# Holding nine instead of five groups of stores behind the loads, with smaller input pools and two groups of K and V in fp32

## The chip, the cores and the metric

The kernel runs on one core of a Trainium2 chip. The metric is the device time of one execution in microseconds; medians of several executions are quoted. A profile gives the span from the core's first to its last instruction, which here is about 1.8 us shorter than the time of the same execution (129.08 against 130.87 us). A ratio always compares with the kernel before as it ran in the same rounds on the same chip; the rounds used several chips.

The names: PE multiplies matrices, DVE and ACT work on vectors, POOL and SP here mostly issue DMA transfers. A DMA issued by POOL stands in the profile under a queue of the kind "software_dynamic"; one issued by SP or ACT under "hardware_dynamic", called a hardware queue below. The profile counts the packets of all queues against the same 16 DMA engines. The traces have sixteen reports of each transfer, read here as one for each engine; a transfer has landed with the last of them.

## The reference, cut to what matters

```python
# Q, K, V: (8, 12, 512, 64) float32
Q_feat = np.maximum(0, Q)
K_feat = np.maximum(0, K)
KV    = np.einsum('bhkd,bhkv->bhdv', K_feat, V)
K_sum = np.sum(K_feat, axis=2)
numerator   = np.einsum('bhqd,bhdv->bhqv', Q_feat, KV)
denominator = np.einsum('bhqd,bhd->bhq', Q_feat, K_sum)
return numerator / (denominator[:, :, :, None] + 1e-10)
```

There are 96 heads in 24 groups of four. A group needs three loads (Q, K, V) of 512 KB each and one store of 512 KB. That is 72 loads and 24 stores, 50.3 MB in all, and little arithmetic per byte.

## The kernel before

The loads are all issued by POOL, and they convert fp32 in HBM to bf16 in SBUF on the way. The exceptions are K and V of group 0, which come unconverted over the hardware queues so that the first group can start early. Stores are issued by SP as soon as a group's result o_sb is ready, except for five groups (17 to 21), whose stores stand in POOL's program after the last load.

```python
HELD = 5
qin = pool("qin", NG); kin = pool("kin", 20); vin = pool("vin", 20)
outp = pool("outp", 10)
# ... cut ...
k_sb[0] = outp.tile([P, R, D], fp32, name="k_first", tag="o_sb")
nc.sync.dma_start(out=k_sb[0]..., in_=Kr[0])
v_sb[0] = outp.tile([P, R, D], fp32, name="v_first", tag="o_sb")
nc.scalar.dma_start(out=v_sb[0]..., in_=Vr[0])
load_q(0)                                  # POOL, as all of load_q, load_kv
make_identity(nc, ident)
for g in range(1, NG - 2):
    load_kv(g); load_q(g)
load_kv(NG - 2); load_kv(NG - 1); load_q(NG - 2); load_q(NG - 1)
# ... cut ...
def store(g, o_sb):
    if NG - 2 - HELD <= g < NG - 2:
        nc.gpsimd.dma_start(out=Or[g], in_=...)      # POOL: behind the loads
    elif g == NG - 1:
        for j in range(2):                           # SP: two halves of 256 KB
            nc.sync.dma_start(...)
    else:
        nc.sync.dma_start(out=Or[g], in_=...)        # SP: at once
```

Of the kernel before, what the change touches and what calls it, by code (L numbers as in the profile page):

```python
# [10 lines left out]
def kernel(  # L11
# [7 lines left out]
    nc = tc.nc  # L19
    B, H, S, D = Q.shape  # L20
    assert D == 64
    P = 128
# [4 lines left out]
    R = S * NHG // P  # L27
    U = R // 2
    NG = NH // NHG
    assert NG * NHG == NH and R == 16  # L30
    HELD = 5

    fp32 = mybir.dt.float32
    bf16 = mybir.dt.bfloat16
# [3 lines left out]
    def pool(name, bufs, **kw):  # L38
        return ctx.enter_context(tc.tile_pool(name=name, bufs=bufs, **kw))

    consts = pool("consts", 1)
    qin = pool("qin", NG)
    kin = pool("kin", 20)
    vin = pool("vin", 20)
    kfp = pool("kfp", 3)
    qtp = pool("qtp", 3)
    rcp = pool("rcp", 4)
    outp = pool("outp", 10)
    pkv = pool("pkv", 1, space=bass.MemoryType.PSUM)
    pqt = pool("pqt", 2, space=bass.MemoryType.PSUM)  # L50
    pou = pool("pou", 2, space=bass.MemoryType.PSUM)
# [1 line left out]
    def rview(X):  # L53
        return X.rearrange("b h s d -> (b h s d)").rearrange("(n p f) -> n p f", p=P, f=R * D)

    Qr, Kr, Vr, Or = rview(Q), rview(K), rview(V), rview(out)
# [13 lines left out]
    q_sb, k_sb, v_sb = {}, {}, {}  # L70

    def load_kv(g):
        k_sb[g] = kin.tile([P, R, D], bf16, name="k_sb")
        nc.gpsimd.dma_start(out=k_sb[g].rearrange("p r d -> p (r d)"), in_=Kr[g])  # L74
        v_sb[g] = vin.tile([P, R, D], bf16, name="v_sb")
        nc.gpsimd.dma_start(out=v_sb[g].rearrange("p r d -> p (r d)"), in_=Vr[g])  # L76

    def load_q(g):
        q_sb[g] = qin.tile([P, U, 2 * D], bf16, name="q_sb")
        nc.gpsimd.dma_start(out=q_sb[g].rearrange("p u f -> p (u f)"), in_=Qr[g])  # L80


    k_sb[0] = outp.tile([P, R, D], fp32, name="k_first", tag="o_sb")
    nc.sync.dma_start(out=k_sb[0].rearrange("p r d -> p (r d)"), in_=Kr[0])
    v_sb[0] = outp.tile([P, R, D], fp32, name="v_first", tag="o_sb")
    nc.scalar.dma_start(out=v_sb[0].rearrange("p r d -> p (r d)"), in_=Vr[0])
    load_q(0)
    make_identity(nc, ident)
    for g in range(1, NG - 2):
        load_kv(g)  # L90
        load_q(g)
    load_kv(NG - 2)
# [79 lines left out]
    def store(g, o_sb):  # L172
        if NG - 2 - HELD <= g < NG - 2:
            nc.gpsimd.dma_start(out=Or[g], in_=o_sb.rearrange("p r d -> p (r d)"))  # L174
        elif g == NG - 1:
            for j in range(2):
                rs = slice(R // 2 * j, R // 2 * (j + 1))
                nc.sync.dma_start(out=Or[g].rearrange("p (r d) -> p r d", d=D)[:, rs],
                                  in_=o_sb[:, rs])
        else:  # L180
            nc.sync.dma_start(out=Or[g], in_=o_sb.rearrange("p r d -> p (r d)"))
# [47 lines left out]
```

## Time and profile before

| | kernel before |
|---|---|
| time, median | 131.06 us (130.79 to 131.24, 3 runs) |
| span of the profiled run | 129.1 us |
| DMA share of the chain of waits | 86% |
| busy: DVE, PE, ACT | 62%, 59%, 40% |

From the profile page of the kernel before: the DMA engines' busy share in tenths, in 40 equal slices of 3.2 us, then the GB/s that they wrote.

```profile
DMA  4999999999999999999999999999999999999972
GB/s 118 305 209 209 211 171 274 277 219 285 229 269 272 226 285 250 245 286 239 258 282 225 275 262 234 285 249 248 285 230 267 273 227 206 212 216 368 388 307 111
```

From the same page, the chain of work that ended last, shares of the span.

```profile
DMA 86%; issue 3%; PE 3%; POOL 2%; DVE 2%; ACT 2%; ACTq 0%; POOLq 0%
```

The kernel is bound by the DMA engines, which have no hole until the last two slices. GB/s count bytes written; a load writes bf16, half of what it reads. So 209 means 418 GB/s read from HBM, and 388 near the end means stores.

Windows of the kernel before: start and end in us, length, busy time of the engines (with instruction counts), granted PE clock, mean DMA share, GB/s. The DMA share adds the times of overlapping packets, so about 1.0 to 1.1 is full.

```profile
5.00:16.00 11.00, 6.20 (x176) 5.21 (x176) 7.23 (x19) 5.21 (x14) 5.59 (x10) 0.98 1.12 210
118.00:122.00 4.00, 3.48 (x79) 2.75 (x76) 2.69 (x10) 2.29 (x6) 0.53 (x1) 0.59 1.02 408
122.00:124.00 2.00, 0.64 (x32) 0.46 (x32) 1.31 (x4) 0.79 (x1) 0.00 (x0) 1.00 0.70 285
124.00:125.00 1.00, 0.00 (x0) 0.00 (x0) 0.93 (x4) 0.00 (x0) 0.00 (x0) 0.87 0.90 365
125.00:126.00 1.00, 0.00 (x0) 0.00 (x0) 0.47 (x1) 0.00 (x0) 0.00 (x0) 0.50 0.74 293
126.00:127.00 1.00, 0.00 (x0) 0.00 (x0) 0.00 (x0) 0.00 (x0) 0.00 (x0) 0.50 0.76 291
```

The first line is loads alone, the second stores, with the end of the last load (it lands at 118.84). From 122 us on the engines are no longer full: they wait for the last groups' results. That slack is what the change is after. A pair of POOL's issues, ten groups apart, gives the price of a group in the middle (timeline; start us, us, engine, line, operation, tile, count, what the engine waited for):

```profile
39.37 0.53 POOL L74 DMA_DIRECT2D k_sb<-in_K_dram  x1 [0.51 <-DMA v_sb<-in_V_dram]
90.39 0.53 POOL L74 DMA_DIRECT2D k_sb<-in_K_dram  x1 [0.57 <-DMA v_sb<-in_V_dram]
```

That is 5.10 us for three loads and one store.

Now the end. From the list of DMA issues of the kernel before: tile, queue, count, KB each, median us from issue to landing.

```profile
out_dram<-o_sb SPq DMA_DIRECT2D x18, 512.0 KB, 6.9
out_dram<-o_sb POOLq DMA_DIRECT2D x5, 512.0 KB, 9.6
```

And the waits of SP's own queue in the kernel before (who waited for whom, us in total, times, longest). L224 is the line where the kernel ends: SP waits there for all landings, then for the other engines.

```profile
SPq L224 <- DMA out_dram<-o_sb: 1.4, 3, 0.6
SPq L224 <- PEq L224: 1.1, 2, 0.6
```

(PEq is PE's sequencer.)

### The profile page before, as it was taken

Reading aid. Unit: us, or ns where it says so; the run is one execution under the profiler, and the core shown is the slowest. Engines: PE = TensorE matmul, PEld = TensorE weight load, DVE = VectorE, ACT = ScalarE, POOL = GpSimd, SP = SyncE. Lnnn points to the kernel's source line nnn. Section 1 sums busy time; section 2 is a strip of 40 time slices with the busy share of each in tenths; the row PEclk is TensorE's granted clock in tenths of the full one; section 3 lists DMA queues with packets and bytes.
Section 4 is the critical chain, followed back from the end, with each engine's and each line's share of the span. In section 5 each row is a group of like instructions: output and inputs, shape, how many; then the busy total and the mean of one; then the engine's idle time right before and its main releaser. Section 6 shows DMA issues by size and latency. Waiting matters only on the chain.

```text
span 129.1 us, 4091 instructions
## 1 busy us (share of the span) xinstructions
PE 76.5 (59%) x1728; PEld 57.0 (44%) x1728; DVE 79.8 (62%) x230; ACT 51.1 (40%) x121; POOL 45.1 (35%) x81
## 2 busy tenths in 40 slices
PE   0068476547576585485675755855756458887610
PEld 0057354425444363364454544633644336665410
DVE  1283775737757558467476584584673849889660
ACT  3027535433345334433543453344335253652700
POOL 6945343133333315224333243152331335311100
PEclk9999955555555555555555555555555555555785
DMA  4999999999999999999999999999999999999972
GB/s 118 305 209 209 211 171 274 277 219 285 229 269 272 226 285 250 245 286 239 258 282 225 275 262 234 285 249 248 285 230 267 273 227 206 212 216 368 388 307 111
DMA packets 13986, 32.23 MB, mean 250 GB/s; under 512 B 1553, under 2 KB 1553, under 8 KB 13969
## 3 DMA queue, kind: packets, MB, share of 16 engines
q0 software_dynamic: 10800, 20.98, 81.7%
q1 hardware_dynamic: 3024, 10.49, 21.7%
q10 hardware_dynamic: 144, 0.52, 1.1%
q8 instruction: 13, 0.21, 0.6%
q14 instruction: 5, 0.03, 0.1%
HBM read 37.75 MB, written 12.58 MB: 390 GB/s over the span
## 4 chain that ended last, share of the span: by engine, by line
DMA 86%; issue 3%; PE 3%; POOL 2%; DVE 2%; ACT 2%; ACTq 0%; POOLq 0%
DMA q_sb<-in_Q_dram 38%; DMA k_sb<-in_K_dram 27%; DMA v_sb<-in_V_dram 21%; ACT qt L139 2%; PE ps_qt L135 1%; PE ps_out L150 1%; DVE o_sb L164 1%; POOL q_sb L80 0%; POOL v_sb L76 0%; POOL k_sb L74 0%; DVE rec L163 0%; POOL ident masks.py:199 0%; DVE den L161 0%; POOL ident masks.py:197 0%; ACTq L139 0%
## 5 line engine op out<-in xcount | busy, mean ns | idle before, releaser
L120 PE MATMUL ps_kv<-vo,kf 64*128 64x65 bf16 x768 | 25.1, 239 | 36.3 <-DVE vo L112 34.4
L120 PEld LDWEIGHTS <-kf 64*128 64x128 bf16 x768 | 21.4, 126 | 42.0 <-DVE vo L112 34.3
L129 ACT CAST kvd<-ps_kv 64x130 bf16<-64x130 f32 x96 | 25.3, 264 | 36.1 <-PE ps_kv L120 34.2
L139 ACT ACTIVATE qt<-ps_qt 128x1024 bf16<-128x1024 bf16 x24 | 24.6, 1023 | 33.8 <-PE ps_qt L135 33.8
L110 DVE TENSOR_SCALAR kf<-k_sb,mask 128x1024 bf16<-128x1024 bf16 x46 | 20.3, 483 | 27.2 <-DMA k_sb<-in_K_dram 27.2
L150 PE MATMUL ps_out<-kvd,qt 128*32 128x130 bf16 x768 | 28.8, 303 | 10.0 <-DVE o_sb L164 6.9
L164 DVE TENSOR_TENSOR o_sb<-ps_out,rec 128x512 f32<-128x512 f32 x48 | 33.2, 692 | 1.7
L80 POOL DMA_DIRECT2D q_sb<-in_Q_dram x24 | 17.2, 715 | 36.0 <-DMA k_sb<-in_K_dram 34.7
L150 PEld LDWEIGHTS <-qt 128*32 128x32 bf16 x768 | 17.4, 127 | 18.8 <-DVE o_sb L164 12.5
L135 PE MATMUL ps_qt<-ident,q_sb 128*128 128x128 bf16 x192 | 24.3, 306 | 0.7 <-DMA q_sb<-in_Q_dram 0.7
L135 PEld LDWEIGHTS <-q_sb 128*128 128x128 bf16 x192 | 18.1, 139 | 5.5 <-issue 4.4
L76 POOL DMA_DIRECT2D v_sb<-in_V_dram x23 | 12.3, 533 | 19.3 <-DMA q_sb<-in_Q_dram 15.0
L74 POOL DMA_DIRECT2D k_sb<-in_K_dram x23 | 12.4, 541 | 11.8 <-DMA v_sb<-in_V_dram 8.9
L112 DVE COPY vo<-v_sb 128x1024 bf16<-128x1024 bf16 x23 | 9.9, 431 | 8.5 <-DMA v_sb<-in_V_dram 8.5
L163 DVE RECIPROCAL rec<-den 128x8 f32<-128x8 f32 x48 | 9.7, 203 | 1.7
L161 DVE TENSOR_SCALAR den<-ps_out 128x8 f32<-128x8 f32 x48 | 7.5, 157 | 1.7 <-PE ps_out L150 1.7
L174 POOL DMA_DIRECT2D out_dram<-o_sb x5 | 2.7, 549 | 7.8 <-DVE o_sb L164 6.2
L110 DVE TENSOR_SCALAR kf<-k_first,mask 128x1024 bf16<-128x1024 f32 x2 | 1.4, 751 | 3.8 <-DMA k_first<-in_K_dram 3.8
L129 ACT ACT_TABLE_LOAD x1 | 1.3, 1283 | 1.8 <-DVE kvd L103 1.8
L101 DVE MEMSET mask<- 32x1 f32 x8 | 0.3, 59 | 0.9 <-PEq L213 0.8
L103 DVE MEMSET kvd<- 128x260 f32 x3 | 0.8, 275 | 0.0
L112 DVE CAST vo<-v_first 128x1024 bf16<-128x1024 f32 x1 | 0.7, 692 | 0.0
(7 smaller groups left out, 1.1 us busy)
## 6 DMA issues: line engine op xcount, KB each, us to landing
out_dram<-o_sb SPq DMA_DIRECT2D x18, 512.0 KB, 6.9
q_sb<-in_Q_dram POOLq DMA_DIRECT2D x24, 256.0 KB, 12.4
k_sb<-in_K_dram POOLq DMA_DIRECT2D x23, 256.0 KB, 13.7
v_sb<-in_V_dram POOLq DMA_DIRECT2D x23, 256.0 KB, 13.7
out_dram<-o_sb POOLq DMA_DIRECT2D x5, 512.0 KB, 9.6
v_first<-in_V_dram ACTq DMA_DIRECT2D x1, 512.0 KB, 4.8
k_first<-in_K_dram SPq DMA_DIRECT2D x1, 512.0 KB, 4.7
out_dram<-o_sb SPq DMA_DIRECT2D x2, 256.0 KB, 2.4
```

The costliest lines, as they stand in the source:

```text
L74: nc.gpsimd.dma_start(out=k_sb[g].rearrange("p r d -> p (r d)"), in_=Kr[g])
L76: nc.gpsimd.dma_start(out=v_sb[g].rearrange("p r d -> p (r d)"), in_=Vr[g])
L80: nc.gpsimd.dma_start(out=q_sb[g].rearrange("p u f -> p (u f)"), in_=Qr[g])
L110: nc.vector.tensor_scalar(kf[g][:, :, s, :], k_sb[g], scalar1=0.0, scalar2=mask[:, s:s + 1], op0=Alu.max, op1=Alu.mult)
L112: nc.vector.tensor_copy(vo[g % NB][:, :, 0:D], v_sb[g])
L120: nc.tensor.matmul(ps_kv[g][:, t, 0:D1], kf[g][ts_, r, :, :].rearrange("p s d -> p (s d)"), vo[g % NB][ts_, r, :], start=(r == 0), stop=(r ...
L129: nc.scalar.copy(kvd[g % NB][64 * c:64 * c + 64, :, s, c, :], ps_kv[g][64 * s:64 * s + 64, :, 0:D1])
L135: nc.tensor.transpose(ps_qt[g][:, u, :], q_sb[g][:, u, :], ident)
L139: nc.scalar.activation(qt[g].rearrange("p u q -> p (u q)"), ps_qt[g].rearrange("p u q -> p (u q)"), Act.Relu)
L150: nc.tensor.matmul(po[hs, v // 2, (v % 2) * 2 * D1:(v % 2) * 2 * D1 + 2 * D1], qt[g][:, u, hs], kvd[g % NB][:, h // 2, h % 2, :, :], start ...
L163: nc.vector.reciprocal(rec, den)
L164: nc.vector.tensor_tensor(o_sb[:, 8 * j:8 * j + 8].rearrange("p (b r) d -> p b r d", b=2), pv[:, :, :, 0:D], rec.unsqueeze(3).to_broadcast ...
```

## The change

Its intent: the time from 122 us on, in which the DMA engines wait for the last results, is to be filled with stores that are ready. So four more groups of stores (13 to 21 instead of 17 to 21) are held behind the loads. The loads end earlier, compute ends earlier, and the held stores cover the wait. Output buffers for this are won by smaller input pools. K and V of group 1 are also loaded in fp32 over the hardware queues.

```diff
-    HELD = 5
+    HELD = 9
+    F32 = 2
...
-    qin = pool("qin", NG)
-    kin = pool("kin", 20)
-    vin = pool("vin", 20)
+    qin = pool("qin", 14)
+    kin = pool("kin", 14)
+    vin = pool("vin", 14)
...
-    outp = pool("outp", 10)
+    outp = pool("outp", HELD + 4)
...
-    k_sb[0] = outp.tile([P, R, D], fp32, name="k_first", tag="o_sb")
-    ... (K[0] on SP, V[0] on ACT)
+    for g in range(F32):
+        ... (the same for g = 0 and 1)
     load_q(0)
     make_identity(nc, ident)
-    for g in range(1, NG - 2):
+    load_q(1)
+    for g in range(2, NG - 2):
         load_kv(g)
         load_q(g)
```

More of the change, by code (lines that the diff above doesn't have):

```diff
@@ L80, in load_q @@
         nc.gpsimd.dma_start(out=q_sb[g].rearrange("p u f -> p (u f)"), in_=Qr[g])
-    k_sb[0] = outp.tile([P, R, D], fp32, name="k_first", tag="o_sb")
-    nc.sync.dma_start(out=k_sb[0].rearrange("p r d -> p (r d)"), in_=Kr[0])
-    v_sb[0] = outp.tile([P, R, D], fp32, name="v_first", tag="o_sb")
-    nc.scalar.dma_start(out=v_sb[0].rearrange("p r d -> p (r d)"), in_=Vr[0])
+    for g in range(F32):
+        k_sb[g] = outp.tile([P, R, D], fp32, name="k_first", tag="o_sb")
+        nc.sync.dma_start(out=k_sb[g].rearrange("p r d -> p (r d)"), in_=Kr[g])
+        v_sb[g] = outp.tile([P, R, D], fp32, name="v_first", tag="o_sb")
+        nc.scalar.dma_start(out=v_sb[g].rearrange("p r d -> p (r d)"), in_=Vr[g])
     load_q(0)
     make_identity(nc, ident)
-    for g in range(1, NG - 2):
+    load_q(1)
+    for g in range(2, NG - 2):
         load_kv(g)
```

## The prediction

> **What bounds the kernel now.** The DMA engines. The slice table shows them at 9 tenths or more from about 3 us to 122 us, with no hole; the chain of waits is 86% DMA, all of it loads of Q, K and V. DVE (62%), PE (59%) and ACT (40%) have room. Cutting the span into 1 us windows gives the prices. Before the first store (5 to 16 us) 209 GB/s are written into SBUF; a load reads fp32 and writes bf16, so 420 GB/s are read, and one load (512 KB read) takes 1.25 us; POOL's issues there are also 1.24 us apart. In the middle a group (three loads, one store) takes 5.10 us (issues of K from 39.4 to 90.4 us, ten groups), so a mixed-in store costs 5.10 - 3.75 = 1.35 us. Stores alone (118 to 122 us) run at about 408 GB/s, 1.29 us each.
>
> So the time is nearly a sum: 72 loads and 24 stores at full rate, plus three losses: the start (by 3 us only 0.28 MB has moved, about 2.3 us lost), the tail, and about 2 us between the last byte (127.1) and the end of the span. In the tail the loads' data ends near 117 us, five held stores run to 122, then from 122 to 127.1 the DMA share is only 0.67 to 0.90 while stores wait for the last two groups' compute (last o_sb at 125.5). Seven stores and 1.5 loads take 12.1 us from 115 us on; at full rate about 10.9. Tail loss: 1.2 to 1.5 us. That is what the change can win.
>
> **What it removes, adds, moves.** No byte of HBM traffic is removed. Four more stores (groups 13 to 16) move behind the loads: loads end 4 x 1.35 = 5.4 us earlier (about 111.5), so the last o_sb is ready near 120 to 121 us; eleven stores then follow, 11 x 1.29 = 14.1 us, to about 125.6. The backlog covers the last groups' compute with some 4 us to spare, so the tail loss should nearly vanish. The moved stores cost 1.29 instead of 1.35 us: 0.25 us more. In the longer load-only stretch DMA needs 3.75 us per group, and DVE needs 3.7 (prep to prep, 105 to 116 us), so compute just keeps pace; a small lag is covered.
>
> 14 input buffers: POOL keeps just 8 transfers outstanding (each issue waits for the landing of the eighth before it), under three groups ahead, so neither 20 nor 14 binds. 13 output buffers: no o_sb waits for a held store.
>
> K1 and V1 in fp32: same bytes read, so about the same DMA time. The Trainium skill (DMA: Bandwidth & Descriptors, "Issuing engines are not separate DMA queues") says all queues share the same 16 engines; this trace agrees: adding SP's stores slows the loads. Gain at the start at most 0.3 us. Cost: group 1's prep is about 0.8 us longer on DVE (751 against 482 ns twice, 692 against 430), hidden.
>
> **Predicted:** span about 127.5, time 129.4 us (-1.3%), range 128.5 to 130.5. Faster by over 2%: 0.10; within 2%: 0.87; slower: 0.03.
>
> **What would show it right:** load-only stretch from about 75 us on at 209 GB/s; last load landing about 5 us earlier; then some 13 us of stores near 400 GB/s at full DMA share; chain of waits ending in a store's DMA instead of DVE o_sb; middle still 5.1 us per group.
>
> **What would make it wrong:** stores alone slower than 400 GB/s when many are queued, or POOL's eight-deep window starving them; DVE not keeping 3.7 us, so that last stores come after 125 us; fp32 loads on hardware queues moving faster or slower than cast loads; a larger gain at the start than 0.3 us.

## The result, and the profile after

| | before | changed |
|---|---|---|
| time, median | 130.93 us (4 runs) | 133.09 us (132.86 to 133.19, 4 runs) |
| span of the profiled run | 129.1 us | 131.3 us |
| ratio to before | | 1.016, 95% interval 1.0134 to 1.0186 |

A ratio is the mean time of one kernel's fast runs over that of the other's of the same rounds, so it is not quite the ratio of the medians quoted. The changed kernel is 1.6% slower, clear of the noise, where 1.3% faster had been predicted. It stays within 2% of the kernel before, to which the prediction gave 0.87, but with the opposite sign and outside the range of 128.5 to 130.5 us, so this is no success of its argument. (The median before is over one run more than in the table above.)

The same slices of the changed kernel (each 3.3 us now):

```profile
DMA  4999999999999999999999999999999999999920
GB/s 119 376 291 209 212 182 280 275 238 270 252 240 283 248 248 284 237 258 273 237 270 264 232 285 255 240 210 210 210 209 210 209 213 240 401 411 418 393 91 0
```

Much of what was planned happened. There is a long stretch of loads alone near 210 GB/s, then stores alone at 393 to 418, with DMA engines full. But the last slice holds no DMA at all, and the one before it little. The windows of the changed kernel show it:

```profile
112.00:124.00 12.00, 5.04 (x112) 3.95 (x112) 5.72 (x16) 3.08 (x6) 1.60 (x3) 0.50 1.03 413
124.00:125.00 1.00, 0.00 (x0) 0.00 (x0) 0.00 (x0) 0.00 (x0) 0.00 (x0) 0.50 0.73 289
125.00:126.00 1.00, 0.00 (x0) 0.00 (x0) 0.00 (x0) 0.00 (x0) 0.00 (x0) 0.50 0.44 174
126.00:127.00 1.00, 0.00 (x0) 0.00 (x0) 0.00 (x0) 0.00 (x0) 0.00 (x0) 0.50 0.15 57
127.00:128.40 1.40, 0.00 (x0) 0.00 (x0) 0.00 (x0) 0.00 (x0) 0.00 (x0) 0.50 0.00 0
128.40:131.00 2.60, 0.00 (x0) 0.00 (x0) 0.00 (x0) 0.00 (x0) 0.00 (x0) 0.50 0.00 0
```

Twelve microseconds at 413 GB/s are what was hoped for. Then two things follow that the prediction did not have. The DMA share decays over 3 us (0.73, 0.44, 0.15) instead of stopping, which means that some of the 16 engines finish much later than others. And from 127.3 us on nothing moves, no engine is busy, and yet the program goes on to 131.25. The waits of SP's queue in the changed kernel (L227 is the end of the kernel):

```profile
SPq L227 <- DMA out_dram<-o_sb: 6.6, 1, 6.6
SPq L227 <- PEq L227: 3.3, 2, 2.8
```

SP waits for the last landing and then 2.8 us more for the other engines, against 0.6 before. PEq is only the name nearest in time: PE had long finished. The trace's own records of the sequencers name the engine that is late. At its end the program has a DRAIN instruction on each engine (prof leaves it out of its views; these times were read from the packed traces). POOL's is the long one: in the changed kernel it begins with POOL's last issue and runs for 15.5 us, against 1.0 us or less on the others:

```
kernel     POOL's last issue   POOL's last landing   POOL's DRAIN ends   SP is done   span
before     119.71              125.19                128.29              127.92       129.08
changed    114.98              127.28                130.46              127.83       131.25
```

(All in us. "SP is done" is the end of SP's DRAIN after its waits for all landings.) In both kernels the span is the later of the two columns before it plus 0.79 us. In the kernel before, POOL's drain already ends last, but only by 0.37 us. In the changed kernel POOL's drain ends 2.6 us after SP is done, and the whole difference of the spans (2.17 us) is the difference of the drains' ends (2.17 us). In these two kernels the drain ends 3.1 to 3.2 us after the last landing on POOL's own queue.

Why does POOL's queue land so late? Its last store was issued early. The last of POOL's held stores in the changed kernel (all operations on the output that start between 114.5 and 115.5 us):

```profile
L177 POOL DMA_DIRECT2D out_dram<-o_sb x1: 533/533/533, 115.0 to 115.0; - x1
DMA to landing us min/median/max: 12.3/12.3/12.3
```

And the last of them in the kernel before (between 119 and 120 us):

```profile
L174 POOL DMA_DIRECT2D out_dram<-o_sb x1: 531/531/531, 119.7 to 119.7; - x1
DMA to landing us min/median/max: 5.5/5.5/5.5
```

With nine held stores and those of the last groups behind the loads, all of this work ends together near 127 us, so POOL's queue, too, lands at the very end. With five it was through 2.5 us before SP's last piece.

### The profile page after: what moved, and what is told of

Same layout as the page of the kernel before. It is cut to its first block, busy times and chain, and to the rows that moved or that the text cites. A ratio compares the mean times of both kernels' runs of the same rounds, so it can differ in the third digit from the quotient of the medians.

```text
span 131.3 us, 4110 instructions
## 1 busy us (share of the span) xinstructions
PE 76.9 (59%) x1728; PEld 57.2 (44%) x1728; DVE 80.2 (61%) x230; ACT 51.3 (39%) x121; POOL 44.6 (34%) x83
## 4 chain that ended last, share of the span: by engine, by line
DMA 76%; DVE 4%; PE 4%; POOL 3%; issue 3%; ACT 2%; ACTq 0%; POOLq 0%
DMA v_sb<-in_V_dram 39%; DMA k_sb<-in_K_dram 20%; DMA q_sb<-in_Q_dram 17%; DVE o_sb L167 2%; ACT qt L142 2%; PE ps_qt L138 2%; PE ps_out L153 1%; POOL k_sb L75 1%; DVE vo L115 1%; PE ps_kv L123 1%; POOL q_sb L81 1%; DVE kf L113 1%; DVE rec L166 0%; POOL v_sb L77 0%; DVE den L164 0%
## 5 line engine op out<-in xcount | busy, mean ns | idle before, releaser
L113 DVE TENSOR_SCALAR kf<-k_sb,mask 128x1024 bf16<-128x1024 bf16 x44 | 19.4, 483 | 18.4 <-DMA k_sb<-in_K_dram 18.4
L81 POOL DMA_DIRECT2D q_sb<-in_Q_dram x24 | 15.6, 648 | 31.5 <-DMA k_sb<-in_K_dram 15.7
L77 POOL DMA_DIRECT2D v_sb<-in_V_dram x22 | 11.7, 533 | 15.5 <-DMA q_sb<-in_Q_dram 9.2
L177 POOL DMA_DIRECT2D out_dram<-o_sb x9 | 4.9, 541 | 6.6 <-DVE den L164 2.4
L113 DVE TENSOR_SCALAR kf<-k_first,mask 128x1024 bf16<-128x1024 f32 x4 | 2.8, 750 | 5.2 <-DMA k_first<-in_K_dram 5.2
L115 DVE CAST vo<-v_first 128x1024 bf16<-128x1024 f32 x2 | 1.4, 696 | 0.0
```

The lines of the kernel that those rows point to most:

```text
L77: nc.gpsimd.dma_start(out=v_sb[g].rearrange("p r d -> p (r d)"), in_=Vr[g])
L81: nc.gpsimd.dma_start(out=q_sb[g].rearrange("p u f -> p (u f)"), in_=Qr[g])
L113: nc.vector.tensor_scalar(kf[g][:, :, s, :], k_sb[g], scalar1=0.0, scalar2=mask[:, s:s + 1], op0=Alu.max, op1=Alu.mult)
L115: nc.vector.tensor_copy(vo[g % NB][:, :, 0:D], v_sb[g])
```

## The experiments

The theory (A): the end of the program waits for a drain of POOL that ends some 3 us after the last landing on POOL's queue, and the change moved that landing from 125.19 to 127.28. The rivals: (B) the other parts of the change, the fp32 loads or the small pools, cost the time; (C) eleven stores behind the loads are too much work after the loads, whichever queue they use.

### HELD back to 5, the rest of the change kept

```diff
-    HELD = 9
+    HELD = 5
-    outp = pool("outp", HELD + 4)
+    outp = pool("outp", 13)
```

> The changed kernel with HELD back at 5 (13 output buffers, 14 input buffers and fp32 K1/V1 kept). Theory A (the end of the program waits for a POOL drain that ends about 3.2 us after the last landing on POOL's queue; the nine held stores moved that landing from 125.2 to 127.3 us): time back to about 131.2 us, 0.2 to 0.4 us over the kernel before because of the slower start; POOL's last landing near 125.4. Rival B (the fp32 loads on the hardware queues or the 14 buffers cost the time): stays near 133.

Measured: 130.82 us against 130.94 for the kernel before, ratio 0.9995 (0.9974 to 1.0016). POOL's last landing is at 125.22, the drain ends at 128.25. The 0.2 to 0.4 us for a slower start that the expectation added did not show. So the number of held stores alone makes the change slower, and rival B falls.

### fp32 loads of group 1 taken back, nine held

```diff
-    F32 = 2
+    F32 = 1
-    load_q(1)
-    for g in range(2, NG - 2):
+    for g in range(1, NG - 2):
```

> The changed kernel with K1 and V1 loaded as before, in bf16 over POOL's queue; nine stores held and 14 buffers kept. Theory A: still 3.1 us of drain after POOL's last landing near 127, time 132.7 to 133.1. Rival B (the fp32 loads cost the 2.1 us): 131.

Measured: 133.24 us, ratio to before 1.0184 (1.0166 to 1.0203), 0.14 us above what theory A expected. POOL's last landing is at 127.47, its drain ends at 130.73. The fp32 loads neither win nor cost anything that these runs resolve.

### Larger input pools, nine held

```diff
-    qin = pool("qin", 14)   kin 14   vin 14
+    qin = pool("qin", NG)   kin 18   vin 18
```

> The changed kernel with 24 Q buffers and 18 each for K and V. Theory A: no change, 132.9 to 133.3; POOL's issues stay at most eight transfers ahead of the landings. Rival (the reuse of 14 buffers delays loads): 131 to 132.

Measured: 133.11 us, ratio 1.0181 (1.0162 to 1.02). The pool sizes do nothing.

### One half-store moved onto POOL's queue in the kernel before

```diff
-                nc.sync.dma_start(...)
+                (nc.sync if j == 0 else nc.gpsimd).dma_start(...)    # last store, halves j = 0, 1
```

> The kernel before, with only the second half of the last store (256 KB) moved from SP to POOL's queue. Theory A: the drain now follows a landing near 127.7 to 128.2 us; the end is that landing + 4.0 us, so span 131.5 to 132.2, time 133.4 to 134.1 us (+2.4 to 3.1 us). Rival C: the data lands when it did, perhaps 0.5 us later; time 131.0 to 131.6.

Measured: 135.33 us, ratio 1.0336 (1.0319 to 1.0353), even more than expected. This is the cleanest sign: 256 KB on another queue, the same bytes, 4.4 us slower. The waits of SP's queue in this run:

```profile
SPq L225 <- PEq L225: 4.7, 2, 4.2
SPq L225 <- DMA out_dram<-o_sb: 3.1, 1, 3.1
```

The landing came at 128.27 us, 0.6 us later than the same half's in the kernel before. The drain ended at 132.78, 4.5 us after that landing instead of 3.1. So the drain's time after the landing is not one constant.

### Both halves of the last store on POOL

```diff
-                nc.sync.dma_start(...)
+                nc.gpsimd.dma_start(...)
```

> The kernel before with both halves of the last store on POOL's queue. Theory A: the drain again ends 3 to 4.5 us after POOL's last landing (128 to 129), time 134.5 to 136. If the gap between landing and end of drain grows with the number of transfers POOL still has in flight, it is longer than the 4.5 us of e5_lastpool; if it is longer when the queue had run empty first, it is nearer 3.1.

Measured: 134.87 us in one run, so its state is unknown and it has no interval. POOL's last landing is at 127.71, the drain ends at 132.31, 4.6 us later. With one more transfer in flight the gap is as in the run before, so it does not grow with their number here. What makes it 4.5 after a half-store and 3.1 after a whole one stays open.

### Nine held on POOL, but groups 11 to 19

```diff
-        if NG - 2 - HELD <= g < NG - 2:
+        if NG - 4 - HELD <= g < NG - 4:
```

> The changed kernel, still nine stores held on POOL's queue, but groups 11 to 19 instead of 13 to 21, so that groups 20 to 23 go out on SP and come last. Same bytes behind the loads. Theory A: POOL's last landing comes 1 to 2.5 us earlier than 127.3, and the span follows it, landing + 4.0 us, or SP's last landing + 1.4 us if that is later: 128.8 to 130.3 us of span, 130.7 to 132.2 of time. Rival C (eleven stores behind the loads are simply too much DMA work after the loads, whichever queue): stays near 133.

Measured: 132.84 us, ratio 1.0148 (1.0126 to 1.0169). The expected earlier landing did not come: POOL's last landing is at 127.10. The time is near what rival C expected, so this run does not part A from C; the runs on SP's queue below do. The span (131.07) is again that landing plus 4.0. The reason for the miss is in two views of single stores of this run. POOL's last store, issued at 112.5:

```profile
L177 POOL DMA_DIRECT2D out_dram<-o_sb x1: 533/533/533, 112.5 to 112.5; - x1
DMA to landing us min/median/max: 14.6/14.6/14.6
```

and SP's last half, issued at 117.5, five microseconds later:

```profile
L181 SPq DMA_DIRECT2D out_dram<-o_sb x1: 332/332/332, 117.5 to 117.5; - x1
DMA to landing us min/median/max: 7.5/7.5/7.5
```

SP's landed at 125.0, POOL's at 127.1. The Trainium skill (DMA: Bandwidth & Descriptors, "Queues, rings and completion order") says that each DMA engine goes round-robin between the queues that have work for it. This trace agrees: SP's half took 7.5 us and passed POOL's store, which took 14.6. Our reading is that SP's stores find a short queue and that each one pushes POOL's long queue back. Holding earlier groups moved POOL's last landing by only 0.2 us: by this reading, because POOL's queue was still full when SP's stores came.

### Held stores on SP: first try, which held nothing

> The changed kernel with the same eleven stores (13 to 23) behind the loads, but all on SP: stores 13 to 19 are put into SP's program after its wait for o_sb of group 20, none on POOL. Theory A: POOL's drain is over long before the end, the span is SP's last landing + about 1.4 us; with the last landing at 126.5 to 127.3 that is 127.9 to 128.7 us of span, 129.8 to 130.6 of time, faster than both kernels. Rival C: the last landing is no earlier than 127.3 and the end costs 4 us as in the changed kernel: 133.

The edit was wrong. In SP's program store 13 stood ahead of store 20, and SP waits in order for each store's own result, so every store left as soon as it was ready. What ran is a kernel that holds no store at all. It took 134.54 us, ratio 1.0276 (1.0247 to 1.0306): the last loads land at 122.80 instead of 113.13, and SP's last half at 131.92. It serves as a measure of what holding is worth. POOL's drain was over at 125.61 and SP's wait for the others is short; the span is SP's end plus 0.76 us.

### Held stores on SP: store 20 first

```diff
+    later = {}                          # before store(); the rest of store() is cut
-        if NG - 2 - HELD <= g < NG - 2:
-            nc.gpsimd.dma_start(out=Or[g], in_=o_sb...)
+        if NG - 2 - HELD <= g < NG - 4:
+            later[g] = o_sb
+        elif g == NG - 4:
+            for n, o in [(g, o_sb)] + list(later.items()):
+                nc.sync.dma_start(out=Or[n], in_=o...)
```

> The run e6_sp held nothing: its SP program put store 13 ahead of store 20, so each store left as soon as its own o_sb was ready. Here store 20 comes first in SP's program and 13 to 19 after it, so eight stores leave together near 110 us. Theory A: POOL's drain ends before 120 us, the span is SP's last landing + about 1.1 us; with the last landing at 126.5 to 127.5, as in the changed kernel, 127.6 to 128.6 us of span, 129.5 to 130.5 of time: 2.5 to 3.5 us under the changed kernel with the same bytes behind the loads. Rival C (the stores' backlog itself costs the time): 133.

Measured: 130.74 us against 130.74 for the kernel before, ratio 0.9998 (0.9976 to 1.0019). The same eleven stores are behind the loads as in the changed kernel, on another queue, and the median is 2.35 us lower (2.2 us when each kernel is taken against the kernel before of its own rounds). Rival C falls. POOL's drain ended at 115.97, and SP's waits at the end (L232) are short:

```profile
SPq L232 <- DMA out_dram<-o_sb: 3.8, 5, 1.3
SPq L232 <- PEq L232: 0.7, 2, 0.5
```

The time is 0.24 us over the range that was expected, because the last landing came at 127.83 and not by 127.5. Windows of this run:

```profile
110.00:111.00 1.00, 0.68 (x28) 0.41 (x21) 1.00 (x3) 0.85 (x4) 0.00 (x0) 0.50 0.89 164
111.00:112.00 1.00, 0.38 (x15) 0.12 (x6) 0.96 (x5) 0.00 (x0) 0.00 (x0) 0.50 0.84 238
```

The loads run out before the stores, which wait for group 20, have reached the engines.

### The same with K1 and V1 in bf16

> e7_sp_held with K1 and V1 in bf16 over POOL's queue as before. Theory A: the start is up to 0.3 us quicker, so the same as e7_sp_held or up to 0.3 us faster: 129.3 to 130.4.

Measured: 130.78 us, ratio 1.0002 (0.9988 to 1.0016). No difference to the run above; again the fp32 loads of group 1 change nothing that these runs resolve. The expected range was missed by 0.4 us, as it had been set before e7_sp_held itself came out at 130.74.

### The same, started by store 19

The edit against e7_sp_held:

```diff
-        if NG - 2 - HELD <= g < NG - 4:
+        if NG - 2 - HELD <= g < NG - 5:
-        elif g == NG - 4:
+        elif g == NG - 5:
```

> e7_sp_held with the held stores (13 to 18) placed behind store 19 instead of store 20 in SP's program, so that they start about 3.7 us earlier, while the last loads still run. In e7_sp_held the DMA share sank to 0.89 and 0.84 between 110 and 112 us; that gap, worth about 0.3 us, should close. Expected 130.3 to 130.7 us against 130.74; if the stores now delay the last loads so much that compute ends late, 131 or more.

Measured: 130.31 us against 130.83, ratio 0.9958 (0.9942 to 0.9973). The gap closed, as expected: the DMA share is 1.07 in both microseconds from 110 to 112, where e7_sp_held had 0.89 and 0.84.

### Two held stores on POOL, early, and six on SP

The edit against e7_sp_held:

```diff
+        if NG - 2 - HELD <= g < NG - HELD:                  # 13 and 14
+            nc.gpsimd.dma_start(out=Or[g], in_=o_sb...)
-        if NG - 2 - HELD <= g < NG - 4:
+        elif NG - HELD <= g < NG - 4:                       # 15 to 19, with 20
             later[g] = o_sb
```

> e7_sp_held with the two earliest held stores (13 and 14) on POOL's queue behind the last load, the other six (15 to 20) on SP as before, started by store 20. Theory A: POOL's last landing is about 115 to 117 us and its drain over by 120, so using POOL's queue for held stores costs nothing when they land early; the two stores fill the DMA gap of e7_sp_held at 110 to 112 us. Expected 130.2 to 130.6 us. If any held store on POOL costs its drain: 133.

Measured: 130.20 us (130.14 to 130.38, 6 runs) against 130.87, ratio 0.9949 (0.9936 to 0.9961). POOL's last landing is at 117.12, its drain ends at 120.02. The gap at 110 to 112 us closed here too (shares 1.11 and 1.09). This is the lowest ratio of a correct run, 0.5% below the kernel before, though its interval overlaps that of e9_trigger19. Its DMA is nearly that of the changed kernel, window by window:

```profile
112.00:124.00 12.00, 5.07 (x112) 3.97 (x112) 5.65 (x16) 3.07 (x6) 0.00 (x0) 0.50 1.03 413
126.00:127.00 1.00, 0.00 (x0) 0.00 (x0) 0.00 (x0) 0.00 (x0) 0.00 (x0) 0.50 0.15 57
```

The rate is 413 GB/s in both, the share between 126 and 127 us is 0.15 in both, and the last landing is at 127.25 against 127.28. Only what follows differs:

```profile
SPq L234 <- DMA out_dram<-o_sb: 6.4, 3, 5.2
SPq L234 <- PEq L234: 0.7, 2, 0.5
```

SP waits 0.5 us for the others instead of 2.8. So two held stores on POOL's queue cost nothing that these runs resolve when they land by 117 us. What costs is a landing on that queue near the end.

### What makes the engines finish apart: fewer instructions (wrong result)

The sixteen reports of one landing were up to 4.9 us apart at the end of the changed kernel (POOL's last store, 4.4 us: first 122.91, mean 124.88, last 127.28). A candidate (D) is the fetching of instructions: the profile page of every run with the full program counts 13 packets in the queue "instruction", 0.21 MB. Each of these packets lasts 0.88 to 1.03 us in the traces of before, changed and e7_sp_held. In e7_sp_held the spread of a landing's reports grew from 1.28 to 2.20 us after the fetch at 114.9.

```diff
-        for r in range(R):              # K-V matmuls
+        for r in (0, R - 1):
```

> Wrong result on purpose: e7_sp_held with 4 of the 32 K-V matmuls of each group, so that the program has 1344 fewer PE instructions of each pair. Theory D (each 16 KB instruction fetch takes 0.9 to 1.0 us of one DMA engine, and with DMA engines full to the end the engine with most fetches lands last): 8 instead of 13 fetches, the spread of the last store's 16 landings falls from 1.7 us to 1.0 or less, the span by 0.4 to 0.7 us. If fetches do not matter: spread 1.7 us and span 128.9 as in e7_sp_held.

(The 1344 are 672 matmuls and their 672 weight loads.)

Measured: 129.76 us, ratio 0.9906 (0.9884 to 0.9927). The fetches fell to 8. The span fell by 0.9 us, more than expected, but the spread only from 1.72 to 1.57 us, where 1.0 or less had been expected. The mean of the last reports moved instead, from 126.45 to 125.71. Five fetches fewer are worth an estimated 0.3 us of mean DMA time (5 x 0.95 / 16, from the packets' times in the traces, if each occupies one engine); the held stores also started 0.7 us sooner (109.94 against 110.68). And the edit changed more than fetches: the granted PE clock was 1.0 in all six runs, against 0.575 to 0.64 in those of e7_sp_held. Inconclusive: one late fetch at 114.7 again came just before a jump in the spread (1.28 to 2.12), but that the fetches cause most of the unevenness is not shown.

### All runs by one rule

```
run             held stores         POOL's last   drain    gap    SP is    later of   span
                                    landing       ends            done     the two
before          5 POOL              125.19        128.29   3.10   127.92   128.29     129.08
changed         9 POOL              127.28        130.46   3.19   127.83   130.46     131.25
e2_held5        5 POOL              125.22        128.25   3.02   127.87   128.25     129.03
e1_f32_1        9 POOL              127.47        130.73   3.27   128.16   130.73     131.51
e3_bufs         9 POOL              127.34        130.52   3.19   127.89   130.52     131.31
e4_early        9 POOL              127.10        130.28   3.19   127.65   130.28     131.07
e5_lastpool     5 POOL + half       128.27        132.78   4.51   128.76   132.78     133.57
e10_both_pool   5 POOL + 2 halves   127.71        132.31   4.60   128.26   132.31     133.10
e6_sp           none                122.80        125.61   2.82   132.24   132.24     133.00
e7_sp_held      on SP               113.15        115.97   2.82   128.16   128.16     128.91
e8_sp_held_f1   on SP               113.31        116.21   2.90   128.31   128.31     129.07
e9_trigger19    on SP               115.66        118.48   2.82   127.78   127.78     128.53
e11_fewer_mm    on SP               112.40        115.22   2.82   127.27   127.27     128.04
e12_mixed       2 POOL, rest SP     117.12        120.02   2.90   127.70   127.70     128.47
```

In all fourteen traces the span is the later of POOL's drain and SP's end, plus 0.76 to 0.79 us. POOL's drain follows its queue's last landing by 2.8 to 4.6 us; SP is done within 0.6 us of the last landing of all.

## Why the prediction was wrong, point by point

- **What bounds the kernel: right.** DMA was and stayed the bound. A group in the middle still takes 5.1 us (POOL's issues of K at 44.20 and 85.28 us in the changed kernel, eight groups apart, give 5.14).
- **Loads end earlier: right.** Predicted 5.4 us; the last load landed at 113.13 instead of 118.84, 5.7 us earlier. The start of the load-only stretch was misplaced: about 75 us predicted, about 85 us seen.
- **Compute keeps up and the backlog covers it: right.** The last o_sb was done at 120.2 us (predicted 120 to 121), and the engines were full from 112 to 124 us.
- **Stores alone at 400 GB/s: right.** 413 were measured.
- **14 buffers, 13 output buffers, fp32 loads: right.** They cost nothing that the runs resolve (e1_f32_1, e2_held5, e3_bufs, e8_sp_held_f1). The gain of up to 0.3 us at the start did not show.
- **"Eleven stores then follow ... to about 125.6": wrong in its last part.** The mean of the 16 engines fits: SP's last half was reported at 125.67 on average. But the program waits for the slowest engine, and POOL's last store was reported by it at 127.28, 1.6 us later and 1.7 us after the 125.6 predicted. The prediction worked with mean rates. In the kernel before, the tail's slack hid the unevenness: the reports of POOL's last store were 2.8 us apart, but the last piece of all was reported by all engines within 0.35 us (127.31 to 127.66). Filling the slack uncovers it; what was called tail loss could only partly be won.
- **"About 2 us between the last byte (127.1) and the end of the span": the step that failed.** It was taken for a constant. It is the later of two things, SP's end and POOL's drain. The drain led by 0.37 us before; the change made POOL's queue land at the very end, and the drain then led by 2.6 us. In the changed kernel the end costs 3.98 us after POOL's last landing (3.19 for the drain, 0.79 for the rest). Without the drain the span would have been about 127.83 + 0.79 = 128.6 us and the time about 130.4 (an estimate from this trace), inside the predicted range; e12_mixed, with nearly the same DMA and an early drain, measured 130.20.

Together: 125.6 predicted for the data, plus 1.7 for the slowest engine, plus 4.0 for the end instead of 2 is 131.3, the measured span. So two steps failed, and the one at the end takes the time out of the range. That the drain sets the end of the changed kernel is shown by moving work between queues (e5_lastpool, e7_sp_held, e12_mixed). What makes the engines uneven, and what sets the drain's length between 2.8 and 4.6 us, is open.

The chain of waits, which the prediction expected to end in a store's DMA, ended in DVE's o_sb in both kernels: it does not follow the end of the program. The waits of SP's queue do. The last line of the chain (start us, us, what), of the kernel before and then of the changed one:

```profile
124.78 0.69 DVE o_sb L164
119.49 0.69 DVE o_sb L167
```

## What to carry to other kernels

Before filling the idle tail of a DMA-bound kernel, look at what happens after the last byte. In this kernel the end can wait for POOL's drain, which ends 2.8 to 4.6 us after the last landing on POOL's queue. So let POOL's queue run out some 5 us before the end and give the last stores to SP. To hold stores behind loads on SP, put them in its program behind a store whose result comes late: SP issued in order in e6_sp and e7_sp_held. And when a tail is filled to the end, reckon with the last of the sixteen reports of a landing, not with their mean (1.6 us between them here).

## What the Trainium skill lacked or had wrong

- DMA: Bandwidth & Descriptors, "Issuing engines are not separate DMA queues", says that issuing from several engines only saves the sequencer's issue time. Here the queue mattered by more: half a store moved from SP to POOL made the kernel 4.4 us slower (e5_lastpool), and the held stores moved from POOL to SP made it 2.2 us faster, each against its own rounds (ratios 1.016 and 0.9998, e7_sp_held). That all queues share the same engines fits e4_early, where POOL's last store took 14.6 us while SP's passed it.
- No page has the drain of POOL at the end of a program with transfers on its queue: 2.8 to 4.6 us after that queue's last landing in fourteen traces, in a kernel where POOL issues nothing more by then. The fixed cost of about 2 us per DMA that "Anatomy of one DMA" gives (DMA: Bandwidth & Descriptors) does not cover it: it comes after the landing.
- The same page says that the 16 engines finish independently and that two of them are usually slower, but gives no size. Here the sixteen reports of one landing on POOL's queue drift 2 to 5 us apart in the course of the kernel (4.4 us for the last store of POOL in the changed kernel, 0.4 us for the first loads of the kernel before), and the tail pays for it. The packed traces do not say which engine reports last.
- Runtime: NRT & Kernel Launch, "Instruction fetch mechanics", has the 16 KiB blocks of 256 instructions; the traces agree roughly (13 packets of 16 KB for 3456 PE instructions, 8 for 2112 in e11_fewer_mm). It calls the cost of crossing a block mostly hidden and gives no time for the fetch itself. In this DMA-bound kernel each packet lasts 0.88 to 1.03 us; what that costs the kernel is not shown (e11_fewer_mm).
